# The decay of b~ and k~ to the chunk's end on DVE instead of POOL, as a step of the written order

## The chip, the cores and the metric

The kernel runs on one core of a Trainium2 chip. The metric is the device time of one execution in microseconds, the median over the runs. Before the change it is 2436.6 us (3 runs, 2434.49 to 2438.38).

## The reference, cut to what matters

A trunk of two layers over 512 tokens of 1024 channels. Each layer is a half-step SwiGLU FFN, a token mixer and another half-step FFN, with a layer norm after each. The mixer of layer 0 is a neighbourhood attention, that of layer 1 a bidirectional RWKV-7 scan with 16 heads of 64 channels. The change touches only the scan:

```
def step(state, inp):
    r_t, w_t, k_t, v_t, a_t, b_t = inp
    sa = einsum('zbhij,zbhj->zbhi', state, a_t)
    state = state * w_t[..., None, :] + sa[..., None] * b_t[..., None, :] + v_t[..., None] * k_t[..., None, :]
    return state, einsum('zbhij,zbhj->zbhi', state, r_t)
_, ys = lax.scan(step, zeros((2, B, H, N, N)), xs)     # z = 2: one scan forward, one on the reversed tokens
```

## The kernel before

The scan is done in chunks of 64 tokens (CH), eight chunks (NC), for a pair of heads (hp, 0 to 7) and both directions (z) at a time. Within a chunk the recurrence is turned into matrix products; for that a, r, b and k are scaled with the running product of the decays (the text calls the scaled ones b~ and k~; they lie in the tile bk, and a~ and r~ in ar). To hand the state on to the next chunk, b~ and k~ have to be decayed further, to the end of their chunk: the tile bk is multiplied by pe, one number per channel and chunk. This product (L1063) is what the change is about. It comes after the products of bk with ar (the Gram matrices), which need bk as it was, and before the transposes of bk into the tiles tb, which need it decayed.

The steps of a pair are generators of the class Scan. A step is what stands between two yields:

- load (token l): DMAs of a pair's inputs. front (f0 and f1 for the two directions): a matmul L985, then the scaled a~, r~, b~, k~.
- grams (g0, g1): for each half of the chunks 16 matmuls L1046 into two PSUM banks; DVE masks them into the tiles xs (L1051); ACT copies the 32x32 diagonal blocks into qd and qc (L1055, L1057); DMAs move the rest. In the kernel before, POOL's product L1063 is issued in the last of grams' steps.
- invert (i): the triangular blocks are inverted by substitution. DVE transposes qd into qs (L1131), a DMA fetches a unit matrix into zs (L1133), and POOL does 31 pairs of small products and sums (L1139, L1141). qs and zs have one buffer each.
- inverted (k): two transposes on DVE (L1151, L1152) bring the inverse back, in qd (then called zc) and in qs (then zt). merge (j, two steps): DMAs of zc into az, and two groups of 64 small matmuls (L1169, L1176), the first of which reads zt.
- tails (t0, t1): PE transposes the decayed bk (L1073), ACT copies it to tb (L1074).
- values (v): nine steps, eight of them one matmul L1087. bonus (b): L1099. turn (n): L1121 and the tile pd (L1110).
- chain (c, 31 steps) and outputs (d): the recurrence over the chunks, with PE, ACT and DVE by turns: L1197, L1204 and L1206, L1210, L1216, L1228, the copy L1218 on DVE.
- finish (x) and gate (e) end a pair; r and o are matmuls of other parts of the layer that fill the first two and the last two slots (L901, L1258).

A slot n works on several pairs at once: chain and outputs of pair n, inverted, merge and turn of pair n + 1, front f1, grams, tails, values, bonus and invert of pair n + 2, load and f0 of pair n + 3. There are ten slots, -2 to 7. The order of the steps within a slot is written out by hand in SEQ: a row of tokens each for the slots -2, -1, 6 and 7, and one (0) for the slots 0 to 5. So an inversion that is issued in slot n is awaited by token k of slot n + 1.

PE, ACT and DVE follow the written order exactly (MANUAL_SCAN, in run). POOL and the DMA queue of SP are not in that set: for them a scheduler places the instructions. Each engine works its own queue in order, so that an instruction that waits holds up all that stand behind it on that engine.

Of the kernel before, what the change touches and what calls it, by code (L numbers as in the profile page):

```python
# [15 lines left out]
ALU = mybir.AluOpType  # L16
AX = mybir.AxisListType

P = 128
# [23 lines left out]
CH = 64  # L43
NC = S // CH
# [13 lines left out]
}  # L58
SEQ = {
# [32 lines left out]
def flat(ap):  # L92
    return ap.rearrange("p a b -> p (a b)")
# [745 lines left out]
class Scan:  # L839
# [193 lines left out]
    def grams(self, hp, z):  # L1033

        k, nc = self.k, self.nc
        p = self.st[hp]
        ar, bk = p.ar[z], p.bk[z]
        own, other, r = HALF[z], HALF[1 - z], z * CH
        for q in range(2):
            x, az = self.take(hp, z, q)[0], p.az[:, :, z * NC + q * 4 : z * NC + q * 4 + 4]  # L1040
            ss, us = slice(q * 4, q * 4 + 4), slice(z * NC + q * 4, z * NC + q * 4 + 4)
            pgs = [k.bank("g") for _ in HALF]

            for j in range(4):
                for h, hs in enumerate(HALF):
                    nc.tensor.matmul(pgs[h][:, j * P : (j + 1) * P], flat(bk[hs, q * 4 + j]), flat(ar[hs, q * 4 + j]),  # L1046
                                     start=True, stop=True)

            mask = self.mask[:, z].rearrange("p (o a) t -> p o a t", o=1).broadcast_to([P, 4, 2, CH])
            for h in range(2):  # L1050
                nc.vector.tensor_tensor(x[:, h], pgs[h].rearrange("p (u a t) -> p u a t", u=4, a=2), mask, ALU.mult)  # L1051
            yield
            for h, hs in enumerate(HALF):
                for d in range(2):
                    nc.scalar.activation(p.qd[h * 64 + d * 32 : h * 64 + d * 32 + 32, us, :],  # L1055
                                         x[r + d * 32 : r + d * 32 + 32, h, :, 0, d * 32 : d * 32 + 32], AF.Copy)
                nc.scalar.activation(p.qc[h * 64 : h * 64 + 32, us, :], x[r : r + 32, h, :, 0, 32:64], AF.Copy)  # L1057
                nc.sync.dma_start(az[own, h], x[own, h, :, 1, :])
                nc.sync.dma_start(x[own, h], ar[hs, ss])
                if q and h:  # L1060

                    bke = bk.rearrange("p s a t -> p s (a t)")
                    nc.gpsimd.tensor_tensor(bke, bke, p.pe[z].broadcast_to([P, NC, 2 * CH]), ALU.mult)  # L1063
                yield

    def tails(self, hp, z):

# [383 lines left out]
```

## Time and profile before

| what | time |
|---|---|
| median of the runs | 2436.6 us |
| profiled execution | 2445.82 us |
| its span | 2444.0 us |
| PE busy | 2251.2 us (92%) |
| DVE busy | 1124.7 us (46%) |
| ACT busy | 986.2 us (40%) |
| POOL busy | 1461.2 us (60%) |

The profiled execution is one of its own: 2445.82 us, of which the span from the first to the last instruction is 2444.0 us. Busy shares are averages over the FFNs, the attention and the scan, which have different limits. The scan lies between about 1508 and 2032 us of the span. Slot 0 begins with the first chain matmul (L1197) at 1607.97 us, slots 1 to 6 at 1652.60, 1706.83, 1757.78, 1816.46, 1874.45 and 1931.83 us.

### The profile page before, as it was taken

The numbers are of one execution on the slowest core, as the hardware profiler recorded it, in microseconds if no ns is written. First come the engines' busy times: TensorE is split into PE (matmuls) and PEld (weight loads), VectorE is DVE, ScalarE is ACT, GpSimd is POOL, SyncE is SP. The second block draws the span as 40 slices with busy tenths as digits, with TensorE's granted clock in tenths as the row PEclk, the third lists the DMA queues.
The fourth block names the chain that finished last, engine by engine and source line by source line (L and its number), as shares of the span: only waits on it lengthen the run. The fifth ranks groups of instructions, "written<-read, shape, count | busy, mean of one in ns | idle before, by whom it ended". The sixth has DMA issues, their size and how long they took to land.

```text
span 2444.0 us, 35030 instructions
## 1 busy us (share of the span) xinstructions
PE 2251.2 (92%) x13664; PEld 1767.7 (72%) x13664; DVE 1124.7 (46%) x1559; ACT 986.2 (40%) x1728; POOL 1461.2 (60%) x1247
## 2 busy tenths in 40 slices
PE   8999999999999999999999697998877794999998
PEld 7888878777888887888887564565555453888886
DVE  2233375454532335623336864465655335333336
ACT  3333343465433333433334344465644323233334
POOL 6788753554577884778875321556655504487863
PEclk9999999999999999999999797999989897999999
DMA  6444443422444445444444356643333315344443
GB/s 194 146 145 138 147 163 115 131 72 75 125 130 146 142 135 188 139 147 146 139 145 157 95 176 238 167 112 106 92 88 101 108 58 189 99 138 139 150 168 120
DMA packets 351361, 330.38 MB, mean 135 GB/s; under 512 B 48554, under 2 KB 277546, under 8 KB 351196
## 3 DMA queue, kind: packets, MB, share of 16 engines
q1 hardware_dynamic: 351196, 328.15, 42.7%
q8 instruction: 107, 1.75, 0.3%
q14 instruction: 58, 0.48, 0.1%
HBM read 263.05 MB, written 48.53 MB: 127 GB/s over the span
## 4 chain that ended last, share of the span: by engine, by line
PE 72%; DVE 10%; POOL 7%; DMA 5%; issue 3%; ACT 2%; SPq 1%; DVEq 0%; POOLq 0%; ACTq 0%
PE bank L198 15%; PE bank L200 15%; PE bank L199 15%; PE bank L665 12%; POOL zs L1141 3%; PE bank L236 3%; POOL tm L1139 3%; DVE x L303 2%; DVE x L370 1%; PE y L901 1%; DVE tmp L300 1%; DVE w L194 1%; PE a L1258 1%; PE g L1258 1%; PE bank L790 1%
## 5 line engine op out<-in xcount | busy, mean ns | idle before, releaser
L194 POOL TENSOR_TENSOR w<-raw,w 128x1024 fp32r<-128x1024 f32 (+2 forms) x203 | 502.4, 2475 | 320.8 <-ACT w L193 320.7
L198 PE MATMUL bank<-xT,w 128*128 128x512 f32 x1416 | 553.8, 391 | 0.0
L199 PE MATMUL bank<-xT,w 128*128 128x512 f32 x1416 | 551.6, 390 | 0.0
L200 PE MATMUL bank<-xT,w 128*128 128x512 f32 x1416 | 551.6, 390 | 0.0
L193 ACT ACTIVATE w<-raw 128x1024 fp32r<-128x1024 f32 (+1 forms) x207 | 218.7, 1057 | 334.2 <-POOL ts L636 138.0
L344 DVE SCALAR_TENSOR_TENSOR ar<-bank,tmp 128x512 f32<-128x512 f32 x88 | 60.9, 691 | 592.4 <-PE bank L200 577.6
L200 PEld LDWEIGHTS bank<-xT,w 128*128 128x128 f32 x1416 | 266.2, 188 | 55.3
L198 PEld LDWEIGHTS bank<-xT,w 128*128 128x128 f32 x1416 | 265.9, 188 | 55.6
L199 PEld LDWEIGHTS bank<-xT,w 128*128 128x128 f32 x1416 | 266.3, 188 | 54.6
L665 PE MATMUL bank<-w,ring 128*128 128x512 f32 x864 | 202.8, 393 | 11.4 <-DVE w L194 10.3
L665 PEld LDWEIGHTS bank<-w,ring 128*128 128x128 f32 x864 | 162.6, 189 | 49.0 <-DVE w L194 13.2
L665 PE MATMUL bank<-wx,an 128*128 128x512 f32 x792 | 187.3, 389 | 0.0
L665 PEld LDWEIGHTS bank<-wx,an 128*128 128x128 f32 x792 | 148.6, 188 | 30.9
L194 POOL TENSOR_TENSOR wx<-ra,wx 128x512 fp32r<-128x512 f32 x132 | 168.1, 1304 | 0.0
L194 DVE TENSOR_TENSOR ring<-ar,ring 128x1024 fp32r<-128x1024 f32 x44 | 128.4, 2919 | 73.9 <-ACT ring L193 73.7
L1139 POOL TENSOR_TENSOR tm<-qs,zs 128x126 f32<-128x126 f32 (+22 forms) x248 | 102.5, 413 | 96.0 <-DMA zs<-in_eye_dram 59.3
L342 ACT ACTIVATE tmp<-bank 128x512 f32<-128x512 f32 x88 | 52.6, 598 | 244.9 <-PE bank L200 244.9
L636 POOL TENSOR_TENSOR ts<-ra 128x512 f32<-128x512 f32 x44 | 58.2, 1322 | 101.8 <-DMA raw<-in_rw_out_dram 93.2
L193 ACT ACTIVATE wx<-ra 128x512 fp32r<-128x512 f32 x132 | 83.1, 632 | 88.9 <-PE bank L665 68.0
L1141 POOL TENSOR_TENSOR zs<-zs,tm 128x126 f32<-128x126 f32 (+22 forms) x248 | 107.2, 432 | 19.4
L194 POOL TENSOR_TENSOR w<-late,w 128x1024 fp32r<-128x1024 f32 x28 | 70.5, 2517 | 79.0 <-ACT w L193 72.0
L198 PE MATMUL bank<-xT,ring 128*128 128x256 f32 (+1 forms) x352 | 102.6, 306 | 8.1 <-ACT xT L193 6.0
(280 smaller groups left out, 3916.6 us busy)
## 6 DMA issues: line engine op xcount, KB each, us to landing
raw<-in_ffn_w_in_dram SPq DMA_DIRECT2D x176, 512.0 KB, 3.8
ra<-in_ffn_w_out_dram SPq DMA_DIRECT2D x44, 1024.0 KB, 4.9
late<-d_late SPq DMA_DIRECT2D x30, 512.0 KB, 4.9
late<-in_ffn_w_out_dram SPq DMA_DIRECT2D x28, 512.0 KB, 4.1
raw<-in_w_qkv_dram SPq DMA_DIRECT2D x24, 512.0 KB, 3.7
d_late<-ts SPq DMA_DIRECT2D x44, 256.0 KB, 3.3
d_late<-ra SPq DMA_DIRECT2D x44, 256.0 KB, 2.0
xs<-ar SPq DMA_DIRECT2D x64, 128.0 KB, 2.3
```

The lines of the kernel that those rows point to most:

```text
L193: self.nc.scalar.activation(h, raw, AF.Copy)
L194: (eng or self.nc.vector).tensor_tensor(l, raw, h.bitcast(F32), ALU.subtract)
L198: nc.tensor.matmul(out, wh, xh, start=start, stop=False)
L199: nc.tensor.matmul(out, wh, xl, start=False, stop=False)
L200: nc.tensor.matmul(out, wl, xh, start=False, stop=stop)
L236: nc.tensor.matmul(acc[t, h], a, u[:, i, h * 512 : (h + 1) * 512], start=first and n == 0, stop=last and n == 2)
L342: nc.scalar.activation(s, pg, AF.Silu)
L344: nc.vector.scalar_tensor_tensor(raw[:, 3:7:3] if j else raw[:, 0:8:7], halves_of(pu), 0.5, halves_of(s), ALU.mult, ALU.mult)
L636: nc.gpsimd.tensor_tensor(t3, r[:, 1, 1], r[:, 0, 1], ALU.subtract)
L665: self.nc.tensor.matmul(acc, lhs, u[:, i], start=bool(first) and m == 0, stop=last and m == 2, skip_group_check=more)
L1139: nc.gpsimd.tensor_tensor(tv, qs[:, s, 0:s].rearrange("p (a o) -> p a o", o=1).broadcast_to([P, s, n]), zs[:, s : s + 1, c0:].broadcast_to ...
L1141: nc.gpsimd.tensor_tensor(zs[:, 0:s, c0:], zs[:, 0:s, c0:], tv, ALU.add)
```

## The change

The product moves from POOL to DVE (L1064 in the changed file, whose lines below SEQ have numbers one higher). It becomes a step of its own at the end of grams, so that g0 and g1 have seven tokens each instead of six, and the rows of SEQ are written anew for the slots -2, -1, 0 to 5 and 6. In the row for 0 to 5 the tails of the first direction (t0) go from the 38th and 39th of 92 places to the 74th and 76th of 94, behind the last g1, with invert (i) between them (72nd before, 75th now); inverted (k) goes from the 57th place to the 42nd, and the two steps of merge (j) from the 67th and 71st to the 50th and 56th. Its core:

```diff
 SEQ = {
-    0: "c v f1 x c x f1 f1 c g0 v c d x f1 g0 v x g0 g0 c c c v c d n e g0 v g0 v c c c f1 l t0 t0 c d f1 l n c c f0 "
-       "c b n v c d f0 g1 c k c g1 g1 c g1 f0 c d g1 j v g1 v j i b c c f0 t1 c f0 t1 f0 c d c c c c d c c c d",
+    0: "c v f1 x c x f1 f1 c g0 v c d x f1 g0 v x g0 g0 c c c v c d n e g0 v g0 v c c c f1 l n v c d k l n c c v c "
+       "f1 j f0 c d g0 f0 j c c b g1 c g1 v g1 c d g1 c c g1 g1 g1 c t0 i t0 b c d t1 t1 c c c f0 c d f0 c c f0 f0 c "
+       "d",
...
@@ class Scan, grams
                 nc.sync.dma_start(x[own, h], ar[hs, ss])
-                if q and h:
-
-                    bke = bk.rearrange("p s a t -> p s (a t)")
-                    nc.gpsimd.tensor_tensor(bke, bke, p.pe[z].broadcast_to([P, NC, 2 * CH]), ALU.mult)
                 yield
+
+        bke = bk.rearrange("p s a t -> p s (a t)")
+        nc.vector.tensor_tensor(bke, bke, p.pe[z].broadcast_to([P, NC, 2 * CH]), ALU.mult)
+        yield
```

The queue of POOL towards the end of an inversion, in slot 3 of the kernel before: tm and zs are the operands of the substitution, and each product L1063 is the decay of one direction's bk.

```order
L1139 TENSOR_TENSOR tm<-qs,zs 128x45
L1141 TENSOR_TENSOR zs<-zs,tm 128x3x15
L1063 TENSOR_TENSOR bk<-bk,pe 128x1024
L1139 TENSOR_TENSOR tm<-qs,zs 128x30
L1141 TENSOR_TENSOR zs<-zs,tm 128x2x15
L1139 TENSOR_TENSOR tm<-qs,zs 128x16
L1141 TENSOR_TENSOR zs<-zs,tm 128x16
L1063 TENSOR_TENSOR bk<-bk,pe 128x1024
```

The same place now, the end of one inversion and the beginning of the next.

```order
L1140 TENSOR_TENSOR tm<-qs,zs 128x45
L1142 TENSOR_TENSOR zs<-zs,tm 128x3x15
L1140 TENSOR_TENSOR tm<-qs,zs 128x30
L1142 TENSOR_TENSOR zs<-zs,tm 128x2x15
L1140 TENSOR_TENSOR tm<-qs,zs 128x16
L1142 TENSOR_TENSOR zs<-zs,tm 128x16
L1140 TENSOR_TENSOR tm<-qs,zs 128x31
L1142 TENSOR_TENSOR zs<-zs,tm 128x31
L1140 TENSOR_TENSOR tm<-qs,zs 128x30
L1142 TENSOR_TENSOR zs<-zs,tm 128x30
```

The two products are gone from POOL's queue: nothing stands between the small operations of an inversion, and the next inversion follows directly.

The queue of DVE in the second half of slot 2 before, from the last copy of a chunk's state (L1218) over inverted (L1151, L1152) to the transpose that opens the next inversion (L1131); xs_... are buffers of the masked Gram matrices.

```order
L1218 COPY vt<-m 64x128 x2
L1051 TENSOR_TENSOR xs_10771<-g,mask 128x512 x2
L1151 STREAM_TRANSPOSE qd<-zs 128x16x16x2
L1152 STREAM_TRANSPOSE qs<-qd 128x512
L1051 TENSOR_TENSOR xs_10755<-g,mask 128x512 x2
L1005 SCALAR_TENSOR_TENSOR ar<-k,cols,e 128x8x63
L1006 TENSOR_SCALAR ar<-k,cols 128x8
L1007 TENSOR_TENSOR ar<-r,e 128x8x64
L1015 SCALAR_TENSOR_TENSOR iv<-k,cols,iv 128x512
L1218 COPY vt<-m 64x128 x2
L1131 STREAM_TRANSPOSE qs<-qd 128x1024
```

The stretch now, first the place of inverted (L1152, L1153), then the end of grams and the transpose L1132; L1064 is the moved product.

```order
L1219 COPY vt<-m 64x128 x2
L1152 STREAM_TRANSPOSE qd<-zs 128x16x16x2
L1153 STREAM_TRANSPOSE qs<-qd 128x512
L195 TENSOR_TENSOR a2u<-a2r,a2u 128x256
L1024 TENSOR_TENSOR e_13056<-iv,e_13056 128x512
L1025 SCALAR_TENSOR_TENSOR bk<-th,e_13056 128x8x64
L1027 TENSOR_TENSOR kz<-kz 128x512
```

```order
L1219 COPY vt<-m 64x128 x2
L1064 TENSOR_TENSOR bk<-bk,pe 128x1024
L1097 SCALAR_TENSOR_TENSOR kz<-r,cols,kz 128x512
L1052 TENSOR_TENSOR xs_10771<-g,mask 128x512 x2
L1219 COPY vt<-m 64x128 x2
L1052 TENSOR_TENSOR xs_10755<-g,mask 128x512 x2
L1064 TENSOR_TENSOR bk<-bk,pe 128x1024
L1132 STREAM_TRANSPOSE qs<-qd 128x1024
```

Inverted stands earlier, ahead of the end of front f1, and the two products of the slot stand behind it: that of direction 0 before the first mask of g1 in this piece, that of direction 1 between the last mask and the transpose that opens the inversion.

The queue of PE around the first tails of slot 2 before: g<-ident,bk are the transposes of the decayed bk, c, m and y the matmuls of the chain.

```order
L1210 MATMUL c<-wr,az_10777 64x64 x4
L1073 MATMUL g<-ident,bk 128x128 x8
L1216 MATMUL m<-vt,tb_10772 64x64
L1216 MATMUL m<-vt,tb_10756 64x64
L1216 MATMUL m<-vt,tb_10772 64x64
L1216 MATMUL m<-vt,tb_10756 64x64
L1228 MATMUL y<-vt,az_10777 64x64 x4
L1121 MATMUL p<-ident,v 128x128 x4
```

The two places now: first the merge (p<-qs and p<-qd) in the middle of the slot, then the tails after the last g1.

```order
L1088 MATMUL a<-xv,wv 128x512
L1211 MATMUL c<-wr,az_10777 64x64 x4
L1170 MATMUL p<-qs,qc 32x32 x32
L986 MATMUL a<-tri,lw 128x128 x4
L1217 MATMUL m<-vt,tb_10772 64x64
L1217 MATMUL m<-vt,tb_10756 64x64
L1217 MATMUL m<-vt,tb_10772 64x64
L1217 MATMUL m<-vt,tb_10756 64x64
L1229 MATMUL y<-vt,az_10777 64x64 x4
L1177 MATMUL p<-qd,qc 32x32 x32
```

```order
L1207 MATMUL y<-vt,xs_10759 64x64
L1211 MATMUL c<-wr,az_10777 64x64 x4
L1074 MATMUL g<-ident,bk 128x128 x8
L1100 MATMUL a<-kz,onesb 128x512
L1217 MATMUL m<-vt,tb_10774 64x64
L1217 MATMUL m<-vt,tb_10760 64x64
L1217 MATMUL m<-vt,tb_10774 64x64
L1217 MATMUL m<-vt,tb_10760 64x64
L1229 MATMUL y<-vt,az_10777 64x64 x4
L1074 MATMUL g<-ident,bk 128x128 x8
```

The transposes of bk stand some 50 rows later in the slot, behind the Gram matmuls of both directions, and the merge matmuls, which need inverted, stand ahead of the Gram matmuls of direction 1 instead of behind them.

## Rows read from the trace of the kernel before

**Rows 1.** The page's chain that ended last, share of the span by line.

```profile
PE bank L198 15%; PE bank L200 15%; PE bank L199 15%; PE bank L665 12%; POOL zs L1141 3%; PE bank L236 3%; POOL tm L1139 3%; DVE x L303 2%; DVE x L370 1%; PE y L901 1%; DVE tmp L300 1%; DVE w L194 1%; PE a L1258 1%; PE g L1258 1%; PE bank L790 1%
```

**Rows 2.** Busy time by stretch: slot 0, and slots 0 to 5 together.

```profile
core 0: us, PE busy (x) PEld busy (x) DVE busy (x) ACT busy (x) POOL busy (x), PEclk, DMA share, GB/s
1607.97:1652.60 44.63, 41.93 (x618) 29.39 (x617) 28.17 (x48) 28.59 (x79) 26.84 (x57) 1.00 0.45 121
...
1607.97:1931.83 323.86, 263.93 (x3706) 185.68 (x3705) 184.34 (x364) 173.37 (x476) 179.31 (x376) 0.92 0.37 101
```

**Rows 3.** Waits in the scan: us in total, times, longest.

```profile
PE g L1073 <- POOL bk L1063: 43.6, 5, 11.8
```

**Rows 4.** Timeline of POOL in slot 3: an inversion's start, the product, its end.

```profile
1753.62 0.24 POOL L1139 TENSOR_TENSOR tm<-qs,zs 128x31 f32<-128x31 f32 x1 [11.55 <-DMA zs<-in_eye_dram]
...
1781.90 1.90 POOL L1063 TENSOR_TENSOR bk<-bk,pe 128x1024 f32<-128x1024 f32 x1
...
1786.11 0.22 POOL L1141 TENSOR_TENSOR zs<-zs,tm 128x16 f32<-128x16 f32 x1
```

**Rows 5.** Timeline of PE in slot 3, the first tails.

```profile
1783.85 1.97 PE L1073 MATMUL g<-ident,bk 128*128 128x128 f32 x8 [9.46 <-POOL bk L1063]
```

**Rows 6.** Timeline of PE at full clock: merge, front, Gram and chain matmuls.

```profile
1741.59 1.20 PE L1169 MATMUL p<-qs,qc 32*32 32x32 f32 x64
1742.72 1.98 PE L1087 MATMUL a<-xv,wv 128*128 128x512 f32 x4
...
1758.17 1.16 PE L985 MATMUL a<-tri,lw 128*128 128x128 f32 x8
...
1766.07 1.16 PE L1046 MATMUL g<-ar,bk 64*128 64x128 f32 x16
1767.16 0.45 PE L1197 MATMUL c<-vt,xs 128*64 128x64 f32 x8
```

**Rows 7.** Timeline of DVE: masks, inverted, and the transpose that opens an inversion.

```profile
1737.42 1.29 DVE L1051 TENSOR_TENSOR xs<-g,mask 128x512 f32<-128x512 f32 x2 [0.84 <-PE g L1046]
1738.63 1.05 DVE L1151 STREAM_TRANSPOSE qd<-zs 128x512 f32<-128x512 f32 x1
1739.72 0.71 DVE L1152 STREAM_TRANSPOSE qs<-qd 128x512 f32<-128x512 f32 x1
...
1803.46 1.25 DVE L1131 STREAM_TRANSPOSE qs<-qd 128x1024 f32<-128x1024 f32 x1 [0.25 <-ACT qd L1055]
```

**Rows 8.** Lines L1063 and L1110: shortest, median and longest in ns.

```profile
L1063 POOL TENSOR_TENSOR bk<-bk,pe x16: 1892/1898/2641, 1527.8 to 1915.5; 128x1024 f32<-128x1024 f32 x16
...
L1110 DVE TENSOR_TENSOR pd<-eye,pc x8: 1219/1225/2866, 1594.8 to 1934.9; 128x1024 f32<-128x1024 f32 x8
```

**Rows 9.** Timeline of POOL in slot 1: three operations of an inversion.

```profile
1658.11 0.79 POOL L1139 TENSOR_TENSOR tm<-qs,zs 128x110 f32<-128x110 f32 x1
...
1666.13 0.43 POOL L1139 TENSOR_TENSOR tm<-qs,zs 128x135 f32<-128x135 f32 x1
1666.64 1.46 POOL L1141 TENSOR_TENSOR zs<-zs,tm 128x135 f32<-128x135 f32 x1
```

**Rows 10.** Timeline of DVE at the same moments.

```profile
1657.97 0.68 DVE L1007 TENSOR_TENSOR ar<-r,e 128x512 f32<-128x512 f32 x1
...
1666.57 1.22 DVE L1110 TENSOR_TENSOR pd<-eye,pc 128x1024 f32<-128x1024 f32 x1
```

**Rows 11.** PE behind two waits: stretch, length, busy (count), granted clock, DMA.

```profile
1729.00:1731.00 2.00, 2.00 (x20) 0.50 0.00 0
1784.00:1792.00 8.00, 8.00 (x62) 0.50 0.13 35
```

**Rows 12.** Timeline of PE at the start of slot 6.

```profile
1932.21 1.12 PE L1258 MATMUL a<-ar,xv 128*128 128x512 f32 x2
1938.59 2.08 PE L1258 MATMUL a<-ar,xv 128*128 128x512 f32 x2 [5.25 <-DMA ar<-in_rw_out_dram]
```

**Rows 13.** Timeline of PE: the last Gram matmuls of slot -1.

```profile
1593.81 1.16 PE L1046 MATMUL g<-ar,bk 64*128 64x128 f32 x16
```

10 rows, old and new, of the table SEQ are left out of this document.

## The prediction

> **What bounds the kernel now.** I read the chain that ended last first. Most of its span is PE in matmuls of the FFNs (L198 to L200), which the change leaves alone, but two lines of POOL stand in it, L1139 and L1141, the substitution of the inversion, with 3% each [rows 1]. They occur only in the scan, so I went on to the busy time by slot. Slot 0 takes 44.63 us with PE busy for 41.93 of them; slots 0 to 5 together take 323.86 us, 54.0 each, at a mean clock of 0.92 [rows 2]. What slot 0 shows is about what a slot costs when PE sets its pace; the other five take some 11 us more each. The waits name the reason: five times PE's transposes of the tails wait for the product L1063 on POOL, 43.6 us in all, 11.8 at most [rows 3]. The timeline of POOL shows why: the product stands near the end of the inversion that began in the slot before. In slot 3 the inversion starts at 1753.62, the product follows at 1781.90, the last operation ends at 1786.33 [rows 4], and PE starts its tails at 1783.85 after 9.46 us of nothing [rows 5]. Behind the wait the clock stands at 0.50, its lower level of 1.2 GHz [rows 11], and the same matmuls take twice as long for a while.
>
> **What goes.** The product on POOL: 16 instructions of 1.90 us [rows 8], and with them PE's wait of 43.6 us [rows 3]. What was hidden behind that wait comes up now, so the 43.6 us are not the gain. I look for what is late next.
>
> **What comes.** Sixteen products on DVE. The trace has none; the nearest row is pd on DVE, the same 128x1024 of two inputs, one of them broadcast: 1.22 us at least and in the median [rows 8]. The ends: 1.22 and POOL's own 1.90. I take 1.25. The product of direction 0 lies beside PE's matmuls of merge and Gram and costs nothing; without that cover it would be 1.25 us. That of direction 1 stands right ahead of the transpose that opens the inversion (the order shows it), so its 1.25 us lie on the loop below.
>
> **The loop that remains.** An inversion of slot n is awaited by inverted (k) of slot n + 1, and merge, Gram and the next inversion stand behind that in the written order. Call T the end of a slot's last Gram matmuls. From there:
> - To the start of the inversion: two masks 1.29, the moved product 1.25, the transpose 1.25 [rows 7], and 0.25 for three hand-overs: 4.05 us. The unit matrix for zs is no later: in the kernel before, 13.2 us pass from the end of inverted (1740.43) [rows 7] to the start of the inversion [rows 4], with a busy DMA queue between; in the changed order 0.15 + 9.35 + 4.05 = 13.55 us pass anyhow.
> - The inversion: in slot 3 it ran 32.71 us, 30.8 without the product [rows 4]. It is not a constant. A POOL operation of 0.43 us took 1.46 beside pd, and one on a smaller tile took 0.79 beside L1007 [rows 9, 10]. Eight such DVE operations with both inputs in SBUF fell into slot 3's inversion. In the new order seven more do (the second half of front f0 and the beginning of the next front stand behind the transpose L1132 now), at some 0.36 us each: 2.5. I take 33.3; the ends are 30.8 (they fall in gaps) and the rival below.
> - Inverted on DVE: from 1738.63 to 1740.43, 1.80 [rows 7], and 0.15 to PE.
> - From the merge to the next T: two merge groups of 1.13, one front group of 1.08, two Gram groups of 1.09, one L1087 of 0.48, and eight chain groups of 0.38 (distances between starts) [rows 6], 9.05, and 0.3 for the chain's own wait: 9.35.
>
> Sum: 4.05 + 33.3 + 1.95 + 9.35 = 48.65 us a slot. PE's own work is that of slot 0, 44.63 [rows 2], so PE waits at the merge for at least 4 us in each slot. I expect the clock to fall there as it did behind the waits before: 0.50 from 1729 to 1731 and from 1784 to 1792 [rows 11]. A stretch of 4 us at half speed costs 2 us of work, and it lies on the loop. So 50.6 us a slot.
>
> **From slot to slot.** In slot -1 the order around the last Gram matmuls is that of before and PE does not wait there, so its T stays at 1593.81 + 1.09 = 1594.9 [rows 13, 6]. Its inversion meets no finish and gate of an earlier pair, four DVE operations fewer at some 0.5: 31.3. Slot 0: T = 1594.9 + 4.05 + 31.3 + 1.95 + 9.35 = 1641.55, with a short wait that I give no loss of clock. Slots 1 to 5: 1641.55 + 5 x 50.6 = 1894.55. After T PE still has 16 chain groups of 0.38, two tails at half of 1.97 each, since that row is at half clock [rows 5], some 2 us for bonus and front (as four L1087), and 1 us of the chain's own waits: 11.1 us. Slot 6 starts at 1905.7 instead of 1931.83: 26 us.
> At the start of slot 6 PE waited 5.25 us for weights whose buffer is ar (from the second L1258 on, 1932.21 + 1.12 to 1938.59) [rows 12], and ran slowly after it, another 2 us. In the new order the second such matmul stands some 5 us later in slot 6, and the DMAs of inverted no longer stand between the copies out of ar and the load. I count the whole 5.25 + 2 = 7.3 as gone; the ends are 0 and 7.3. Slots -2, 6 and 7 are otherwise PE's work, and none of it is added: 0, give or take 2.
> Gain: 26.1 + 7.3 = 33.4. The profiled execution took 2445.8 us (span 2444.0 and 1.8 around it), so 2412.4 by its own count; it stands 9 us above the median of the runs, 2436.6, and I take the same difference off that: 2403.
>
> **A rule that speaks against the change.** The stretched POOL operation beside pd lasted 1.46 us instead of 0.43 [rows 9, 10]. The Trainium skill (SBUF — State Buffer, Who interferes with whom) says that a DVE instruction with two SBUF inputs and a GpSimd instruction that reads SBUF hold each other off by an exclusive lock for the whole instruction. The trace agrees in kind, but beside L1007 only about half of its length was lost. By the rule's full length the time would be that of rival 3, where it is worked out from rows.
>
> **Rivals.**
> 1. The inversion is hidden, and PE sets the pace: each slot at slot 0's 44.63. For it: at slot 0's pace 44.63 - 4.05 - 1.95 - 9.35 = 29.3 us pass between the opening of an inversion and its inverted, close to the 30.8 of one. Against: the seven operations more. Slot 6 at 1607.97 + 6 x 44.63 = 1875.8, a gain of 56 + 7.3: 2373.
> 2. The loop as above, but without a loss of clock and with an inversion of 31: 46.4 us a slot; T of slot 0 (29.0 for its inversion) at 1639.3, of slot 5 at 1871.3, slot 6 at 1882.4, a gain of 49.4 + 7.3: 2380. It needs a wait of PE too short to lower the clock.
> 3. Each of the 15 DVE operations holds POOL for its whole length: 14 x (0.68 - 0.36) and 0.2 for pd, 4.7 us more an inversion [rows 9, 10]. Slots of 55.3, T of slot 0 at 1646.2 and of slot 5 at 1922.7, slot 6 at 1933.8, 2 us late, less the 7.3: 2431. For it: pd's operation on POOL was stretched by nearly all of pd's 1.22. Against: L1007's was not.
> 4. Slower: PE's wait at the merge keeps the clock low to the next T. Then 9.35 us of the loop take 18.7, a slot 58.0. T of slot 0 is 1651 and of slot 5 1941, slot 6 starts at 1953, 21 us late, less 7.3: 2450. For it: in slot 3 the low stretch was 8 us long [rows 11]. Against: that cost 4 us, not 9, behind a wait of 9.46 [rows 5]. It decides from a low stretch of some 17 us a slot on.
> 5. The move does nothing: PE's wait only changes its name. That needs a slot of 54.0 and slot 6's wait unchanged: 2437.
>
> **How the numbers follow.** Forecast 2403, with 2393 to 2413 of its own: 0.56. Rivals 1 and 2 together: 0.25. Rival 3: 0.11. Rival 4: 0.04. Rival 5: 0.04. A difference under 0.2%, 5 us, is what a measurement of this kernel can't tell from none. Faster by more than that: 0.56 + 0.25 + 0.10 = 0.91; same 0.05; slower 0.04. The range leaves out part of rival 1 and of 3, and 4 and 5: 2374 to 2426.
>
> **What would show it.** The wait of the tails for L1064 is gone or below 2 us in all; DVE's inverted waits for POOL in slots 0 to 5, and PE's merge waits for DVE, 4 to 8 us each; the inversions last 31 to 34 us without a gap between their operations; the moved product takes 1.2 to 1.9 us; slots of 48 to 52 us; no wait over 2 us for weights at the start of slot 6. I am wrong if slots come at 45 us with no wait at the merge (rival 1), if the inversions exceed 36 us (3), or if the clock stays at 0.50 up to the last Gram group (4).

## The result and the profile after

The changed kernel takes 2420.9 us (median of 4 runs, 2415.5 to 2424.6) beside 2437.5 us of the kernel before (4 runs on the same chip): a ratio of 0.9931, 95% interval 0.9909 to 0.9953, so faster by 11 to 22 us. That lies inside the predicted range and 17.9 us above the predicted 2403; the gain is half of the forecast one. The profiled execution takes 2424.63 us, its span 2422.8, 21.2 us less than before.

Where the span went, by stage, first of the kernel before: the part up to the first Gram matmuls of the scan, slots -2 and -1 from there, then slots 6 and 7 and the part behind the scan (slots 0 to 5 between them are [rows 2]). The columns are stretch, length, PE busy (count), granted clock, DMA share, GB/s.

```profile
0.00:1517.27 1517.27, 1439.67 (x6814) 0.98 0.44 141
1517.27:1607.97 90.70, 89.68 (x481) 0.97 0.62 181
...
1931.83:2028.89 97.06, 83.64 (x946) 0.94 0.19 60
2028.89:2444.00 415.11, 374.30 (x1722) 0.94 0.45 147
```

The same stages of the changed kernel, with its slots 0, 1, 2 and 5 by themselves, then slots 0 to 5 together.

```profile
0.00:1514.32 1514.32, 1441.02 (x6814) 0.98 0.44 141
1514.32:1609.98 95.66, 92.36 (x480) 0.93 0.60 173
1609.98:1652.10 42.12, 40.58 (x617) 1.00 0.45 114
1652.10:1705.67 53.57, 46.06 (x622) 0.87 0.43 110
1705.67:1756.82 51.15, 43.65 (x622) 0.93 0.36 92
...
1859.22:1910.29 51.07, 43.41 (x612) 0.90 0.48 139
1609.98:1910.29 300.31, 261.05 (x3707) 0.93 0.41 108
1910.29:2004.06 93.77, 83.48 (x947) 0.95 0.20 65
2004.06:2422.80 418.74, 373.66 (x1722) 0.95 0.45 146
```

Slots 0 to 5 give back 23.6 us and slots 6 and 7 another 3.3. Slots -2 and -1 take 5.0 us more. What lies outside the scan, which the change does not touch, differs by 0.7 us in sum (3.0 less ahead of it, 3.6 more behind). Four of the slots last 51.1 to 51.2 us at a clock of 0.90 to 0.93, and slot 1 lasts 53.57 at 0.87.

The waits in slots 0 to 6 (us in total, times, longest) have turned over against [rows 3].

```profile
DVE qd L1152 <- POOL zs L1142: 35.1, 6, 6.7
PE p L1170 <- DVE qs L1153: 30.1, 6, 5.9
```

The tails wait no more. DVE's inverted waits for POOL's inversion, and PE's merge for inverted, 5.9 us in each of slots 1 to 5. The inversion that corresponds to [rows 4], on POOL:

```profile
1749.29 0.24 POOL L1140 TENSOR_TENSOR tm<-qs,zs 128x31 f32<-128x31 f32 x1 [17.68 <-DMA xs<-ar]
...
1782.55 0.22 POOL L1142 TENSOR_TENSOR zs<-zs,tm 128x16 f32<-128x16 f32 x1
```

It runs from 1749.29 to 1782.77, 33.5 us without a gap. The transpose L1132 that opens it ends at 1749.16; the row names a DMA, but in the next two slots the same wait of 17.7 us is put down to that transpose. The moved product, where [rows 8] had POOL's 1898 ns (shortest, median, longest in ns):

```profile
L1064 DVE TENSOR_TENSOR bk<-bk,pe x16: 1215/1216/1226, 1526.0 to 1900.6; 128x1024 f32<-128x1024 f32 x16
```

PE's clock behind the merge wait, as in [rows 11], first in slot 2 and then in slot 1:

```profile
1733.50:1736.00 2.50, 2.42 (x66) 0.50 0.27 46
...
1738.00:1740.00 2.00, 2.00 (x78) 0.74 0.29 49
1740.00:1742.00 2.00, 2.00 (x42) 1.00 0.65 216
...
1680.00:1685.00 5.00, 4.99 (x88) 0.50 0.25 43
1685.00:1691.00 6.00, 6.00 (x111) 0.50 0.58 165
```

After the same wait the lower level lasts some 5.5 us in one slot and 11 us in another. Slot 1 is 2.4 us longer than slot 2 for this reason alone: PE is idle for 7.5 us in both.

Waits on PE that the forecast did not have, one in slot -1 and two at the start of slot 6 (there [rows 12] had the wait for weights, which is gone):

```profile
1596.64 1.97 PE L1074 MATMUL g<-ident,bk 128*128 128x128 f32 x8 [3.30 <-DVE bk L1064]
...
1914.85 0.74 PE L1217 MATMUL m<-vt,tb 128*64 128x64 f32 x8 [1.71 <-ACT vt L1212]
...
1916.37 1.00 PE L1122 MATMUL p<-ident,vr 128*128 128x128 f32 x4 [0.40 <-ACT vt L1124]
```

The first has its cause on DVE, seven rows earlier: a step of front waits for a DMA that reads ar, and pd, the masks and the product stand behind it in DVE's queue.

```profile
1590.49 0.74 DVE L1006 SCALAR_TENSOR_TENSOR ar<-k,cols,e 128x504 f32<-128x504 f32 x1 [5.06 <-DMA xs<-ar]
...
1595.37 1.22 DVE L1064 TENSOR_TENSOR bk<-bk,pe 128x1024 f32<-128x1024 f32 x1
```

The same delay holds back the inversion of slot -1. Its last Gram matmuls begin at 1589.44, so T, with the 1.09 us of the forecast, is 1590.5; the inversion starts 8.7 us later.

```profile
1589.44 1.16 PE L1047 MATMUL g<-ar,bk 64*128 64x128 f32 x16
```

```profile
1599.20 0.54 POOL L1140 TENSOR_TENSOR tm<-qs,zs 128x31 f32<-128x31 f32 x1 [5.72 <-issue]
```

In the kernel before, this way was long already: from T at 1594.9 [rows 13] it took 7.0 us.

```profile
1601.88 0.24 POOL L1139 TENSOR_TENSOR tm<-qs,zs 128x31 f32<-128x31 f32 x1 [2.94 <-issue]
```

### The profile page after: what moved, and what is told of

It reads as the page before. It is cut to its first block, busy times and chain, and to the rows that moved or that the text cites. A ratio compares the mean times of both kernels' runs of the same rounds, so it can differ in the third digit from the quotient of the medians.

```text
span 2422.8 us, 35000 instructions
## 1 busy us (share of the span) xinstructions
PE 2251.6 (93%) x13664; PEld 1771.4 (73%) x13664; DVE 1139.5 (47%) x1575; ACT 984.7 (41%) x1728; POOL 1438.8 (59%) x1231
## 4 chain that ended last, share of the span: by engine, by line
PE 73%; DVE 10%; POOL 7%; DMA 4%; issue 3%; ACT 2%; SPq 1%; DVEq 0%; ACTq 0%; POOLq 0%
PE bank L199 15%; PE bank L201 15%; PE bank L200 15%; PE bank L666 12%; POOL zs L1142 4%; POOL tm L1140 4%; PE bank L237 3%; DVE x L304 1%; DVE x L371 1%; DVE tmp L301 1%; PE g L1047 1%; DVE w L195 1%; PE y L902 1%; PE m L902 1%; PE g L1259 1%
## 5 line engine op out<-in xcount | busy, mean ns | idle before, releaser
L1140 POOL TENSOR_TENSOR tm<-qs,zs 128x126 f32<-128x126 f32 (+22 forms) x248 | 107.7, 434 | 167.7 <-DVE qs L1132 105.5
```

The costliest lines, as they stand in the source:

```text
L1140: nc.gpsimd.tensor_tensor(tv, qs[:, s, 0:s].rearrange("p (a o) -> p a o", o=1).broadcast_to([P, s, n]), zs[:, s : s + 1, c0:].broadcast_to ...
```

## The experiments

Medians with their ratios to the kernel before, which ran beside each of them on the same chip (2438 to 2440 us), and from each profile the sum of slots 0 to 5 and the span.

| kernel | median us | ratio (95%) | slots 0 to 5 | span |
|---|---|---|---|---|
| the changed kernel, again (a_again) | 2424.0 | 0.9936 (0.9914 to 0.9958) | 300.2 | 2422.1 |
| old order, product on DVE (e2) | 2413.5 | 0.9898 (0.9869 to 0.9926) | 296.6 | 2407.4 |
| new order, product on POOL (e3) | 2448.8 | 1.0031 (1.0016 to 1.0046) | 322.1 | 2448.5 |
| half an inversion (e4) | 2372.7 | 0.9725 (0.9708 to 0.9742) | 255.5 | 2369.2 |
| later tails in slot -1 (e1) | 2430.3 | 0.9956 (0.9942 to 0.9970) | 313.6 | 2432.4 |
| transpose before product (e5) | 2434.4 | 0.9980 (0.9969 to 0.9990) | 318.2 | 2433.0 |
| wait filled with 11 matmuls (e6) | 2428.3 | 0.9962 (0.9948 to 0.9976) | 312.7 | 2433.3 |
| wait filled with 6 (e8) | 2414.1 | 0.9895 (0.9876 to 0.9914) | 292.5 | 2413.2 |
| e2, inverse in zs (e7) | 2445.1 | 1.0033 (1.0016 to 1.0049) | 340.4 | 2447.1 |
| e2, unit matrix early (e9) | 2410.8 | 0.9883 (0.9863 to 0.9902) | 292.2 | 2412.6 |
| e9, product earlier (e10) | 2407.3 | 0.9868 (0.9849 to 0.9887) | 288.4 | 2407.0 |
| e10, copy of the state first (e11) | 2394.5 | 0.9824 (0.9805 to 0.9843) | 272.5 | 2389.0 |

### Engine or order: e2 and e3

e2 leaves SEQ as it was before, and puts the seventh token of grams, the product on DVE, right behind the sixth:

```diff
-   ... c d n e g0 v g0 v c c c f1 l t0 t0 ...
+   ... c d n e g0 v g0 g0 v c c c f1 l t0 t0 ...
```

> Only the engine is changed: the order of the kernel before, with the product on DVE as a seventh step right behind the sixth of g0 and of g1. Theory (the loop inversion, inverted, merge, Gram, transpose, inversion sets the slot): no wait of the tails, the loop has 15 us from inverted to the next inversion as in the kernel before, plus 33 of inversion, 48 us a slot instead of 51.2, and no loss in slot -1; the wait of slot 6 for weights stays: 2405. Rival (the new order is what made the gain): not below 2421, slots of 51 us or more.

e3 keeps the new order and gives the product back to POOL:

```diff
-        nc.vector.tensor_tensor(bke, bke, p.pe[z].broadcast_to([P, NC, 2 * CH]), ALU.mult)
+        nc.gpsimd.tensor_tensor(bke, bke, p.pe[z].broadcast_to([P, NC, 2 * CH]), ALU.mult)
```

> Only the order is changed: the changed kernel's order with the product on POOL. Theory of the loop: the products stand in POOL's gap between two inversions, that of direction 1 costs 1.9 instead of 1.2 us and 0.2 for a hand-over, some 0.9 us in each of five slots: 2425. Rival (the gain is the engine's): the tails wait for POOL again, 2437.

The engine alone gains 26 us and ends 8 us above the 2405 of its theory. The order alone loses 9 (4 to 11 by its interval): on POOL the product still falls inside an inversion, and now it delays inverted, for which the merge waits up to 7.5 us. The two waits of e2 in slots 0 to 5 that matter, on POOL and on PE:

```profile
POOL tm L1134 <- DMA zs<-in_eye_dram: 96.1, 6, 18.6
...
PE g L1068 <- DVE bk L1058: 9.6, 6, 1.9
```

and e3's merges, with the product in the middle of the inversion that the merge of slot 1 awaits:

```profile
PE p L1170 <- DVE qs L1153: 35.1, 6, 7.5
```

```profile
1682.60 1.89 POOL L1064 TENSOR_TENSOR bk<-bk,pe 128x1024 f32<-128x1024 f32 x1
```

Both comparisons point the same way: the change's new order gives back part of what its engine gains. e3 fell 24 us short of its expectation: with the product on POOL the loop through the inversion is longer than the one that the change leaves. By the profiles its slots 0 to 5 are about as long as those of the kernel before (322.1 and 323.9 us), so one wait took the place of another there. The 9 us do not lie in them: slots -2 and -1 take 2.8 us more and what follows slot 5 takes 3.1 more; where the rest lies is not shown.

### The loop: e4

The substitution is cut to half, so the output is not the reference's; everything else is the changed kernel.

```diff
-        for s in range(31, 0, -1):
+        for s in range(31, 15, -1):
```

> The changed kernel with the inversion cut to its first 16 of 31 steps (the inverse is left unfinished, so the output is not the reference's). Theory of the loop: the inversion falls to some 18 us, PE no longer waits at the merge, slots 1 to 5 fall from 51.2 to 43-45 us: 2384. Rival (the denser DVE queue or the written order of PE sets the slots): DVE's and PE's work is the same, 2421 and slots of 51 us.

Measured: 2372.7 us, 48 to 51 less than the changed kernel, and no wait of the merge. Slots 2 to 4 last 43.0 us at full clock. That is PE's own pace, and the difference to 51.2 is what the inversion costs each slot.

### Slot -1: e1

```diff
-        "g1 g1 f0 n i t1 t1 v f0 r v v r v v v b",
+        "g1 g1 f0 n i v f0 r v v r t1 t1 v v v b",
```

> The changed kernel, but in slot -1 the tails of direction 1 (t1 t1) stand four steps later, as they did before. In the profile of the changed kernel slots -2 and -1 took 95.7 us instead of 90.7; the tails of slot -1 waited 3.3 us for the product on DVE and PE ran slowly behind it. If that is where the 5 us went: slots -2 and -1 back to 91 us and the time near 2416. If it is only noise or something else in these slots (the memset on POOL, the late front): 2421, unchanged.

The wait of 3.30 us went and slots -2 and -1 shrank from 95.66 to 89.16 us, but the end did not come earlier: slot 0 grew from 42.12 to 53.19.

```profile
1603.93:1657.12 53.19, 46.13 (x617) 0.84 0.40 103
```

```profile
1630.57 1.92 PE L1170 MATMUL p<-qs,qc 32*32 32x32 f32 x64 [6.24 <-DVE qs L1153]
```

PE reached slot 0's merge earlier, waited 6.24 us there for the same inversion, and the low clock came on top. The wait in slot -1 had cost nothing by itself; it only chose where PE waits. The expectation was a miss: the median is 6 to 9 us above the changed kernel's, with intervals that overlap.

### The product's place: e5, beside the changed kernel once more

```diff
-   ... c c g1 g1 g1 c t0 i t0 b ...
+   ... c c g1 g1 i g1 c t0 t0 b ...
```

> The changed kernel itself, once more, beside the three that follow. Every theory expects its 2421 us, give or take 3; it is the measure for the other three on the same chip.

> The changed kernel, with the transpose that opens the inversion (token i) put ahead of the product of direction 1 in the row of slots 0 to 5. The product of 1.22 us then leaves the loop mask, product, transpose, inversion, inverted, merge, Gram. Loop theory: slots 1 to 5 shorten by 1.2 us of loop each and, where the wait of the merge shrinks from 5.9 to 4.7 us, by some of the clock's loss: 50.0 instead of 51.2, in all 5 x 1.2 and up to 2 more, 2413 to 2416 beside 2421. Rival (the place of the product is not on the loop, because a DMA of a unit matrix into zs holds the inversion back until after it): no change, 2421, and the inversion begins no earlier against the last mask.

Both theories missed. On DVE in slot 2 the transpose now stands first, but waits for ACT's copy of the diagonal blocks into qd:

```profile
1752.12 1.25 DVE L1132 STREAM_TRANSPOSE qs<-qd 128x1024 f32<-128x1024 f32 x1 [1.07 <-ACT qd L1056]
1753.29 1.18 DVE L1064 TENSOR_TENSOR bk<-bk,pe 128x1024 f32<-128x1024 f32 x1
```

```profile
1753.50 1.07 POOL L1140 TENSOR_TENSOR tm<-qs,zs 128x31 f32<-128x31 f32 x1 [20.25 <-DVE qs L1132]
```

From the last Gram matmul (T) to the inversion's start it takes 3.83 us in both kernels: 1749.67 to 1753.50 here, 1745.46 to 1749.29 in the changed one. In the changed kernel ACT's last copy into qd ends at 1747.88 and the product at 1747.98: the product had lain beside the copy, and taking it out of the loop gained nothing. Now it lies beside POOL's first operation, which takes 1.07 us instead of 0.24, and the merge waits 5.9 us as before. What made slots 1, 2 and 4 over 54 us is the clock, again of the two lengths seen above:

```profile
1735.00:1745.00 10.00, 9.78 (x184) 0.50 0.43 112
...
1747.00:1749.00 2.00, 2.00 (x24) 1.00 0.15 40
```

### The clock behind the wait: e6 and e8

Both put matmuls that nobody needs into the wait of the merge, e6 eleven, e8 six:

```diff
-        p1 = k.bank("p").rearrange("p (u t) -> p u t", t=32)
+        pb = k.bank("p")
+        if 2 <= hp <= 6:
+            for _ in range(11):                          # e8: range(6)
+                nc.tensor.matmul(pb, k.ident, self.xv[:, 0, :], start=True, stop=True)
+        p1 = pb.rearrange("p (u t) -> p u t", t=32)
```

> The changed kernel with 11 matmuls of 128x512 that nobody needs, put into merge's own PSUM bank ahead of its first group for the pairs 2 to 6 (the start of the group overwrites them), so that PE works through most of the 5.9 us in which it waited for inverted. They add about 11 x 0.22 = 2.4 us of work at the high clock and twice that at the low one, which fit into the wait. Theory that the lower clock behind the wait costs time on the loop: slots 2 to 5 gain 2 to 2.7 us each, slot 1 up to 5, 2407 to 2412 beside 2421. Rival (the low clock lies beside other waits and costs nothing, so the loop alone sets 51.2): 2421, or a few us more where the added matmuls end later than inverted.

> The changed kernel with 6 matmuls of 128x512 that nobody needs ahead of merge's first group for the pairs 2 to 6, not 11: the 11 took 9.7 us (22 instructions at full clock) and outlasted the wait of 5.9 us, so that they cost what they took. Six take 5.3 us and end before inverted does. Theory that the wait itself sets 48.9 us a slot (PE's 43.0, as in the kernel with half the inversion, and 5.9) and the low clock behind it the other 2.3 us in slots 2 to 5 and 4.7 in slot 1: slots of 49 us, 12 to 14 us less than the changed kernel, 2407 to 2412 beside 2422 to 2424. Rival (the low clock costs the end nothing): 2420 to 2425.

e6 shows a size that I had wrong: eleven such matmuls are 22 instructions and 9.7 us, not 2.4, so that PE came late.

```profile
1731.85 9.71 PE L1170 MATMUL p<-xv,ident 128*128 128x512 f32 x22
```

e8 is the clean test. Its six take 5.4 us and leave a wait of 0.46; slots 1 to 4 are:

```profile
1656.54:1705.37 48.83, 46.73 (x634) 1.00 0.38 98
1705.37:1754.20 48.83, 46.73 (x634) 1.00 0.38 104
1754.20:1802.99 48.79, 47.90 (x634) 0.97 0.42 110
1802.99:1851.81 48.82, 46.74 (x635) 1.00 0.37 97
```

Useless work makes the kernel 7 to 10 us faster than the changed one; the intervals touch at their edges (0.9876 to 0.9914 beside 0.9909 to 0.9953), and the slots are clear of each other. 48.8 us is the loop at full clock; the rest of the 51.2 and 53.6, 2.4 and 4.8 us, was the low clock. The forecast had 48.65 for it. The end gained less than the 15 us of slots 1 to 5: slots -2 to 0 took 139.6 us instead of 137.8 (in e1 142.4), and the part ahead of the scan was 2.6 us longer.

### Opening the loop: e7, e9, e10 and e11

All start from e2. e7 gives zs two buffers, frees qs early, and writes the opening of an inversion (i) ahead of inverted (k):

```diff
-   ... c k c g1 g1 c g1 f0 c d g1 j v g1 g1 v j i b ...
+   ... c c g1 g1 c g1 f0 c d g1 v g1 g1 i v k j b j ...
-        zs = tile_("zs", [P, 32, 16])
+        zs = tile_("zs", [P, 32, 16], 2)
-        p.zc, p.zt = p.qd, qs...
+        p.zc, p.zt = p.qd, zs...
```

> The written order of the kernel before (tails early, product on DVE as a step right behind the masks of its direction), but with two buffers for zs, the inverse's second transpose written into zs instead of qs, and the transpose that opens an inversion (token i) written ahead of inverted (k). The wait for inverted is then off the chain of merge, Gram and mask: an inversion of slot n starts from masks that no longer stand behind inverted of the same slot, and the loop is POOL's own, about 33.3 us of inversion and 2 us around it, shorter than PE's 44.6 us a slot. Loop theory: slots 0 to 5 at PE's pace, 44 to 47 us, 265 to 282 in all instead of 300, and 2385 to 2400 us. Rival (something else sets 50 us a slot, such as the tails' wait for DVE of 1.9 us or the clock): 2410 to 2414, as with the old order and the product on DVE (2413.5).

This made it slower than the kernel before, 2445 us, with the longest slots of all, 58 us at a clock of 0.79:

```profile
1654.84:1712.94 58.10, 51.40 (x621) 0.79 0.33 90
```

```profile
1750.40 1.00 DVE L1146 STREAM_TRANSPOSE qd<-zs 128x512 f32<-128x512 f32 x1
```

```profile
1752.29 1.65 PE L1164 MATMUL p<-zs,qc 32*32 32x32 f32 x64 [4.55 <-POOL tm L1134]
```

POOL had finished each inversion long before and stood idle for up to 30 us. Inverted (L1146) now stood at the end of the slot in DVE's queue, behind masks, front, product and the transpose of the next inversion, and the merge waited for it, 25.3 us in six waits. The order made a new wait; neither theory had seen it.

e9 instead keeps e2's order and fetches the unit matrix a slot earlier:

```diff
@@ grams
+        if z == 0:
+            p.zs = self.tile("zs", [P, 32, 16], 2)
+            nc.sync.dma_start(p.zs, self.eye)
@@ invert
-        zs = tile_("zs", [P, 32, 16])
-        nc.sync.dma_start(zs, self.eye)
+        zs = p.zs
```

> The old order with the product on DVE, and the DMA of the unit matrix into zs taken from the end of the slot to the beginning of the pair's Gram products, a slot earlier, into the second of two buffers. In the old order POOL's inversion waited for this DMA: in slot 3 the transpose into qs ended at 1789.5, the issue of the DMA stood in SP's queue until 1793.2 behind eight copies of the inverse, and POOL began at 1796.7. Theory that this 7 us lies on the loop of the old order (inversion 33.2, inverted, mask, transpose): the inversion begins at the end of the transpose, the loop falls to 43 to 45 us, and PE's pace decides, 43.0 and the tails' wait of 1.9 us: slots of 45 to 47 us instead of 49.4, 2388 to 2400 beside 2413.5. Rival (the tails' wait for DVE and the low clock behind it set the 49.4, the inversion only follows): the inversions begin earlier, the slots stay at 49, 2410 to 2415.

The inversions started earlier, and the slots fell only from 49.4 to 48.7 on the mean: the rival was nearer. What is left in e9 is not the inversion, for which the merge waits once, 1.4 us, but PE's small waits at the slot's end and its clock (0.91 over the six slots). e10 and e11 go after these.

```diff
@@ e10
-   ... c d n e g0 v g0 g0 v c c c f1 l ...
+   ... c d g0 n g0 g0 v e v c c c f1 l ...
@@ e11
-   ... t1 c f0 t1 f0 c d c c c c d c c c d
+   ... t1 c f0 t1 c d f0 c c c c d c c c d
```

> The kernel before this one, and in the row of slots 0 to 5 the product of direction 0 two places earlier, ahead of the gate's two operations of 0.75 us on DVE, so that the tails' transposes wait 0.4 us instead of 1.9. Theory: another 1 to 1.5 us a slot and less of the low clock, 44 to 46 us a slot, 2382 to 2394. Rival (the loop of the inversion sets the slot): the wait of 1.9 only moves to the merge or to the chain, the same time as without it.

> The kernel before this one, and at the slot's end the step c (whose copy of the state on DVE releases the next chunk's matmuls) ahead of the last step f0 of front, in the row of slots 0 to 5. In the kernel before, this copy stood behind two operations of front of 0.7 us, PE waited 1.1 us for it in most slots, and in slots 0, 1 and 3 the clock fell to 0.50 around the slot's end for 8 to 12 us. Theory (what is left over PE's own 43.0 us is these small waits and the low clock they bring): the 1.1 us fall to 0.4 or less, the low stretch is shorter or gone, slots of 44 to 46 us and 265 to 278 in all instead of 288.4, 2390 to 2400 beside 2407. Rival (the clock falls all the same, by the other waits of 0.4 us at the slot's end, where nothing but the chain is left for PE): slots of 47 to 48, 2403 to 2408.

In e10 the tails wait 0.5 us in all, but the gain over e9 is 3 us, with intervals that overlap, where the theory had 17 or more. The clock still falls at the end of slots 0, 1 and 3, where PE waits for DVE's copy of the state; the third row is the end of slot 2, where the same waits leave it at 1.00:

```profile
PE c L1194 <- DVE vt L1215: 9.0, 10, 1.1
```

```profile
1694.00:1698.00 4.00, 2.88 (x36) 0.87 0.68 181
1698.00:1702.00 4.00, 3.63 (x47) 0.50 0.71 207
...
1742.00:1746.00 4.00, 2.87 (x44) 1.00 0.56 138
```

In e11 the copy goes first. The sum of this wait halves, and the clock stays at 1.00 through all six slots:

```profile
1648.01:1694.12 46.11, 42.95 (x622) 1.00 0.44 115
1694.12:1740.06 45.94, 42.95 (x622) 1.00 0.42 111
...
1604.23:1876.71 272.48, 254.91 (x3706) 1.00 0.45 121
```

```profile
PE c L1194 <- DVE vt L1215: 4.3, 5, 1.0
```

One step moved by one place is worth 13 us, and nearly all of it is the clock. Over the six slots PE's idle time fell only from 18.2 to 17.6 us, since other waits grew by nearly what this one lost; its busy time for the same matmuls fell from 270.2 to 254.9. The three low stretches of e10 last 10 to 13 us each, which at half the clock is an estimated 16 us of work. e11 beats both kernels, 2394.5 us, 26 to 30 less than the changed one. It is still 3.0 us a slot above PE's 43.0.

## Why the prediction was right and wrong

The mechanism was right. The tails' wait went, inverted waits for POOL and the merge for inverted, 5.9 us (forecast 4 to 8), and the slots come at the pace of a loop mask, transpose, inversion, inverted, merge, Gram. Halving the inversion (e4) shows that it is the inversion that PE waits for. The product takes 1.22 us on DVE (1.25), the inversion 33.5 (33.3), and the loop at full clock 48.8 (48.65, by e8).

The sizes were too favourable, and that the time lies in the range is owed to the range's width. Of the 33.4 us, the two profiles show 21.2, and the medians 16.6. The steps that failed are three terms of the sum, first of them the clock's loss; what they measured, and the two differences named behind them, add up to the 16.8 us that are missing.

- **The clock's loss in the sum of the loop, "+ 2.0":** 5.6 us too little over slots 1 to 5. From T of slot 0 to T of slot 5 it took 258.6 us instead of 253. e8 shows the loss as 2.4 us in slots 2 to 5 and 4.8 in slot 1, together 14.4 instead of 10. The forecast took one length of the low stretch for all slots, though [rows 11] already held a short and a long one.
- **"I count the whole 5.25 + 2 = 7.3 as gone" at slot 6:** 4.0 too much. The wait for weights went, but the chain's copies on ACT stood behind the gate's there, PE waited 1.71 and 0.40 us, and slots 6 and 7 gave 3.3 us.
- **The 4.05 us from T to the inversion, taken for slot -1 too:** 2.1. T of slot -1 did not stay: counted from the first Gram matmuls of the scan it came 1.4 us earlier than in the kernel before. But from there to the inversion it took 8.7 us, because DVE's queue was late by a DMA; the kernel before had 7.0 there, which its trace showed and the forecast did not use. The inversion was 1.4 us shorter than the 31.3 of the forecast, and T of slot 0 came 2.1 us late. The tails right behind the last product brought the wait of 3.30 us and with it most of the 5.0 us of slots -2 and -1, of which slot 0 gave 2.5 back by reaching its merge when the inversion was almost done. e1 shows that the remedy in slot -1 is worth nothing.
- **Outside the scan:** 0.7 us. From T of slot 5 to slot 6 it was 0.2 us less than forecast.
- **From the profile to the median:** 4.6 us. Before's profiled execution stood 8.3 us above its median of these runs, the changed kernel's 3.7. "The same difference" was not the same; which execution was profiled is chance.

One term was wrong without harm: the product of direction 1 was counted into the loop with 1.25 us. By e5 it lies beside ACT's copy into qd; that copy ends where the product ends, so the 4.05 us from T to the inversion came out as 3.83. I had read DVE's queue there and not ACT's, whose copy [rows 7] names as the releaser of that transpose.

Of the rivals, the first two (2373 and 2380) needed a slot near PE's pace; e4 and e11 show what that takes, a shorter inversion or no loss of clock. The third, that every DVE operation with two inputs holds POOL for its whole length, did not come: 33.5 us for an inversion, not 38. The Trainium skill (SBUF — State Buffer, Who interferes with whom) speaks of an exclusive lock for the whole instruction. In e5 POOL's operation began 0.21 us after the product of 1.18, and its 0.24 us became 1.07, so 0.83 of the 0.97 that were left were lost. Read the same way, L1007 had 0.54 us left in [rows 9, 10] and some 0.4 were lost: that is more than the "about half" of the prediction. That POOL's operations often meet only the rest of DVE's may be what kept the inversion short of 38 us; it is not tested. No run here shows more than the length of the DVE operation. The fourth, a low clock up to the next T, is what slot 1 and e5 came near: 11 us of the lower level instead of 5.5 (its slot 6 adds up to 1952, not 1953). That one wait of 5.9 us ends now in one, now in the other is measured; what decides between them is not settled by these runs.

What the forecast did not ask is whether the new order is needed. It is not: e2, which moves the product and leaves the order, takes 2413.5 us, 7 to 10 less than the change (the intervals overlap at the edge, 0.9909 to 0.9926, so that e2 is no slower is shown, and that it is faster is likely). And the new order brought a loop that does not set the pace in the old one: there the merge waits 3.9 us in all, and an earlier start of the inversions (e9) shortened the slots by 0.7 us.

## What to carry to other kernels

When a wait is taken away, add up the loop that comes up behind it with the engine at full clock, and then put the lower clock on top as a range, not as one number: here a wait of 5.9 us cost 2.4 us more in some slots and 4.8 in others. Change the engine and the order in separate kernels, for one may pay for the other. Where PE is at 93% and waits only for a microsecond at a time, look for the copy that stands one place too late in another engine's queue: the small wait is cheap, the clock that can fall behind it is not.

## What the runs showed of the hardware

- Work that nobody needs can make a kernel faster: 5.4 us of matmuls in a wait of 5.9 us kept the granted clock at 0.97 to 1.00 and saved 2.4 to 4.8 us a slot (e8).
- In e10 a wait of 1.13 us and, within some 7 us, two of 0.37 stand at the end of slots 0 to 4. Behind three of them the clock fell to 0.50 for 10 to 13 us, behind those of slots 2 and 4 it stayed at 1.00; what decides is not shown. With the first wait moved away it stayed at 1.00 for 272 us (e11).
- A 128x512 matmul of f32 by the unit matrix counts as two instructions and took 0.88 us in e6, at a clock of 1.00.
- The same product of 128x1024 takes 1.22 us on DVE and 1.90 on POOL, so the move also shortens the work.
